# Unused bytes between the SBUF pools of a two-block transformer kernel

## The chip, the cores and the metric

The kernel runs on one core of a Trainium2 chip. The metric is the device time of one execution in microseconds (us), from the start of the program to its end; less is better.

## The reference

The program computes two transformer blocks on 256 tokens of 1024 channels, in float32. Cut to the parts that take the weights:

```python
def first_block(x, ...):
    for layer in range(2):
        h = rmsnorm(x, norm_mix[layer])
        if layer == 0:
            mix = nsa_attention(h, a_w_in, ...)          # compressed, selected and windowed attention
        else:
            kv = rmsnorm(x, kv_norm) @ kv_w              # keys and values of three dilated groups
            mix = dilated_attention(h, b_w_q, k_shared, v_shared, b_w_out, rel_bias)
        x = x + mix
        x = x + swiglu(rmsnorm(x, norm_ffn[layer]), ffn_w_up[layer], ffn_w_down[layer])
    return rmsnorm(x, final_norm)

def second_block(x, mem, ...):
    x = x + 0.5 * swiglu_ffn(rms_norm(x, ffn1_norm), ffn1_w_in, ffn1_w_out)
    h = rms_norm(x, mix_norm)
    ... = jnp.split(h @ w_in, offsets, axis=-1)          # indexed attention, S5 state space, memory attention, gates
    merged = g0 * (o_a @ w_o_a) + g1 * glu(y_s @ w_glu) + g2 * (o_mem @ w_o_m)
    x = x + merged @ w_out
    x = x + 0.5 * swiglu_ffn(rms_norm(x, ffn2_norm), ffn2_w_in, ffn2_w_out)
    return rms_norm(x, final_norm)

def swiglu(h, w_up, w_down):                             # 1024 -> 2 x 2816 -> 1024
    a, b = jnp.split(h @ w_up, 2, axis=-1)
    return (jax.nn.silu(a) * b) @ w_down
```

## The kernel before

The residual stream stays in SBUF, transposed: eight tiles `x0` to `x7` of 128 channels by 256 tokens. A weight product runs on TensorE with float32r operands. To keep float32 accuracy both factors are split into a high and a low part, and each block of 128 input channels costs three matmuls, in `mm3`, lines 222 to 224: high weights by high activations, high weights by low activations, low weights by high activations. Nearly everywhere the weights are the stationary operand (128 by 128) and the activations move (128 by 256). In six products (the values of the attentions and of the memory) it is the other way round: the activations are stationary, and 256 columns of weights move (304 in one product).

Weights come from DRAM in blocks of 8 x 128 rows by 256 columns into the pool `raw` (four buffers, SP's DMA queue, line 172). `split` makes the two parts out of such a block, half a block at a time: ScalarE writes the high part `wh` (line 181), VectorE the low part `wl` (line 182), each into one of four buffers of the pool `wsplit`. The two parts of the activations are in the pool `xsplit` (tags `xh`, `xl`, which the attention outputs `oh`, `ol`, `oah`, `omh` and the merged tiles `mgh`, `mgl` share with the normed stream), with two exceptions. The hidden tiles of a feed-forward, `hh` and `hl`, are in a pool that is opened for that feed-forward (`hid`), and the output tiles of the S5 layer, `ysh` and `ysl`, are in a pool of the mixer.

The stages run in this order: `nsa` (layer 0's attention), `ffn0`, `dil` (layer 1's attention), `ffn1`, `ffn1_2` (the second block's first feed-forward), `mix` (the mixer), `ffn2_2`, and the last norm. Within a stage the order of instructions on an engine is written by a planner from the order in the source and from a priority that the norms are given. The squares' sums of a norm are added on POOL (line 287).

A pool's tiles lie one after the other, and the pools one after the other, in the order in which they are opened. Tiles of a few bytes are rounded up to 32. Per partition, the allocation of the kernel before is, in bytes:

```
const    16512    constants, gains, ones and so on
xres     21728    x0 .. x7                              8 x 1024
xsplit   29920    xh0, xl0, xh1 ..   two buffers each  32 x 1024
raw      62688    weights as loaded                     4 x 8192
wsplit   95456    wh 4 x 4096, wl 4 x 4096
tmp     128224    sqacc, sq, R, and six tiles of 32 (6 x 32 = 192)
then    135584    the pools of nsa, then hid of ffn0, then the pools of dil
late    135584    opened after dil: memory, state space constants (13472 in all)
hid     149056    of ffn1, of ffn1_2 and of ffn2_2, one after the other in time
```

In every `hid` the tiles are 1024 bytes each and start with those of the gate; in `ffn1_2` two tiles of 32 bytes stand ahead of the hidden tiles as well (`gg`, `ss2`). Since a weight tile's blocks are 512 bytes apart, and the tiles of xsplit and hid 1024, the address of a moving tile less that of a weight tile is, modulo 512, the same for all matmuls of a product. Only in the product of 304 columns the blocks of weights are 1216 bytes apart.

Of the kernel before, what the change touches and what calls it, by code (L numbers as in the profile page):

```python
# [18 lines left out]
P = 128  # L19
# [7 lines left out]
AHEAD = 400  # the norms' place before the products that are traced earlier  # L27
BEHIND = 100
WARM = 12
NU = 384  # a row of position biases  # L30
# [86 lines left out]
def flipped(t):  # L117
    """[p, 256] with the tokens of each block of 128 backwards."""
    return blocks(t)[:, :, ::-1]


class Builder:
    def __init__(self, ctx, tc, A):
        self.ctx, self.tc, self.nc, self.A = ctx, tc, tc.nc, A
        nc = self.nc
        e = ctx.enter_context
        self.cpool = e(tc.tile_pool(name="const", bufs=1))
        self.xpool = e(tc.tile_pool(name="xres", bufs=1))
        self.xs_pool = e(tc.tile_pool(name="xsplit", bufs=2))
        self.raw = e(tc.tile_pool(name="raw", bufs=4))  # L130
        self.wsp = e(tc.tile_pool(name="wsplit", bufs=4))
        self.tmp = e(tc.tile_pool(name="tmp", bufs=2))
        self.mm = e(tc.tile_pool(name="mm", bufs=2, space=PSUM))
        self.sc = e(tc.tile_pool(name="sc", bufs=2, space=PSUM))
        self.tr = e(tc.tile_pool(name="tr", bufs=2, space=PSUM))
        self.ov = e(tc.tile_pool(name="ov", bufs=2, space=PSUM))
        self.uid = 0
        self.turn = 0
        self.wide = True

        self.vec = self.cpool.tile([P, NVEC], F32, name="vec")
        self.gains = self.cpool.tile([P, KD * len(GAINS)], F32, name="gains")
        nc.scalar.dma_start(self.gains, A["vec"][:, :KD * len(GAINS)])
        self.con = self.cpool.tile([P, NCON], F32, name="con")
        self.ident = self.con[:, COFF["ident"]:COFF["ident"] + P]
        self.ones = self.cpool.tile([P, P], F32, name="ones")
        nc.vector.memset(self.ones, 1.0)
        self.mhalf = self.cpool.tile([P, 16], F32, name="mhalf")
        nc.gpsimd.memset(self.mhalf, -0.5)
        # the array's clock is released by activity  # L150
        for _ in range(WARM):
            nc.tensor.matmul(self.bank("mm")[:, :P], self.ones, self.ones, start=True, stop=True)

    def rest(self):
        """The small inputs that the first products do not wait for."""
        self.nc.sync.dma_start(self.con, self.A["con"])
        self.nc.sync.dma_start(self.vec, self.A["vec"])

# [26 lines left out]
    def units(self, w, K, c0, cols=256, step=8):  # L185
        """H and L blocks of W[:, c0:c0+cols] as stationary tiles, one list per 128 columns."""
# [13 lines left out]
    def ahead(self, units):  # L200
        """The same units, the first of them loaded and split here."""
        first = next(units)
        return itertools.chain([first], units)

    def wide_units(self, w, K, c0, cols):
        """H and L blocks of W[:, c0:c0+cols] as moving tiles."""
        res = []
        n = 1024 // cols
        for k0 in range(0, K // P, 2 * n):
            kb = min(2 * n, K // P - k0)  # L210
            v = self.load(w, k0 * P, kb, c0, cols)
            for k in range(0, kb, n):
                m = min(n, kb - k)
                res += self.split(v[:, k:k + m, :], m, cols)
        return res

    def mm3(self, ps, pairs):
        """Sum of stationary^T moving over the pairs ((sH, sL), (mH, mL))."""
# [10 lines left out]
    def take(self):  # L229
        """The next bank for a product; while self.wide, the attention's banks are free and take turns."""  # L230
# [6 lines left out]
    def proj(self, unit, X):  # L237
        """[128, 256] in PSUM."""
# [10 lines left out]
    def split_act(self, src, name, k, pool=None, flip=False):  # L249
        """src [128, 256] (SBUF or PSUM) into its two parts; flip: src has each block's tokens backwards."""  # L250
# [14 lines left out]
    def gsplit(self, x, g, k):  # L265
        """The two parts of x g, g [128, 1]."""
# [10 lines left out]
    def sq_add(self, acc, x, k, scale=1.0):  # L277
        """acc: the running sum of squares and the last tile's squares, apart."""
# [10 lines left out]
    def sq_sum(self, ps, acc):  # L289
        """The tokens' sums of squares -> ps [128, 2]."""  # L290
# [4 lines left out]
    def rms(self, ss):  # L295
        """(ss / D + eps) ** -0.5, [128, 2]."""
# [7 lines left out]
    def rows(self, r):  # L304
        """[128, 256] in PSUM: each token's r on every partition."""
# [10 lines left out]
    def rstd(self, acc):  # L316
        """(R [128, 256]: each token's rstd on every partition; r [128, 2]: token-major)."""
# [5 lines left out]
    def norm_all(self, xs, gains):  # L323
        """Splits of every x tile for each gain, and the rstd."""
# [11 lines left out]
    def norm_twice(self, pool, xs, first, second):  # L336
        """The splits for a norm of x normed (x itself becomes that), and both rstds' product.

        x r1 g1 r2 g2: the gains go into the splits, r1 r2 into the product, and
        r2 comes from sum((x g1 r1)^2) = r1^2 sum((x g1)^2)."""  # L340
# [26 lines left out]
    def ffn(self, xs, gain, w_up, w_down, factor, between=None, after=None):  # L367
        nc, tc = self.nc, self.tc
        with tc.tile_pool(name=self.n("hid"), bufs=1) as hp:
            if after:  # L370
# [35 lines left out]
    def bias_rows(self):  # L406
        """Rows u[h, i] = -(bias of distance 255 - i), masks added, into DRAM."""
# [23 lines left out]
    def bias_tile(self, pool, u, row0, heads, tag, bufs):  # L431
        """T[p, h, j] = u[row0 + h, p + j]: the biases of query 127 - p of a block."""
# [6 lines left out]
    def pv_transposed(self, pt_pool, Pm, i, width=384):  # L439
        """Transposes of a head's probabilities [128, 128 | 256] -> [keys, 256 | 128]."""  # L440
# [12 lines left out]
    def pv_mm(self, O, i, V, pt, start, stop):  # L453
        """O[64 i + d, q] += sum over keys; V: (block 0, block 1) [128 keys, 64]."""
# [8 lines left out]
    def key_parts(self, pool, ps, R, dst):  # L463
        """Keys of two groups, each group's two parts on both halves of the array; dst(gp) -> views [128, 2, 128]."""
# [12 lines left out]
    def query_parts(self, pool, ps, Rn, tags):  # L477
        """Queries of two heads, scaled, flipped: a head's two parts on the two halves of the array."""
# [13 lines left out]
    def nsa(self, xs, first):  # L492
# [6 lines left out]
        with ExitStack() as es:  # L499
# [3 lines left out]
            # columns: block, branch (selected, windowed), key  # L503
# [63 lines left out]
            # the compression: keys in columns 0..59, values in columns 64..123 of the array  # L567
# [105 lines left out]
            def values(g, st, j):  # L673
                # normalise and gate
# [146 lines left out]
    def exp_exact(self, pool, dst, x, n, tag):  # L821
        """exp(x) to float32's accuracy, [128, n]."""
# [16 lines left out]
    def s5_consts(self, pool):  # L839
        """Discretised system, per state [128, 8]: rotation (cos, sin), magnitude, input factors."""  # L840
# [45 lines left out]
    def s5_prepare(self, keep):  # L886
        """From the weights alone: rotation tables and input matrices into DRAM, output matrices kept."""
# [5 lines left out]
        self.s5_zc = keep.tile([P, 8, 3, 32], F32, name="s5zc")  # Re C, -Re C, -Im C  # L893
# [6 lines left out]
        with tc.tile_pool(name="s5pre", bufs=1) as pool:  # L900
# [10 lines left out]
            for a in range(2):  # L911
                sl = slice(4 * a, 4 * a + 4)
                # input matrices, zero-padded to all 128 channels of the half
# [18 lines left out]
                # rotation tables cos(theta t), sin(theta t)  # L932
# [28 lines left out]
    def s5(self, pool, ypool, us):  # L961
        """us: two [128 channels, 256] -> gelu(y), split."""
# [3 lines left out]
        for a in range(2):  # L966
# [3 lines left out]
            for b in range(4):  # L970
# [21 lines left out]
                # back: xr = c zr - s zi, xi = s zr + c zi; their sums in the products with C  # L992
# [40 lines left out]
    def mem_keys(self, keep):  # L1033
        """Normed keys of the memory, block-diagonal by head pairs."""
# [14 lines left out]
    def head_ss(self, ps, col, x):  # L1049
        """Sums of squares of both halves of x [128, 256] -> ps[:, block, col:col + 2]."""  # L1050
# [15 lines left out]
    def head_rows(self, pool, r, col):  # L1066
        """[128 (2 x 64), 256] in PSUM: rstd of both heads along the tokens."""
# [9 lines left out]
    def mixer(self, xs):  # L1077
# [4 lines left out]
        with ExitStack() as es:  # L1082
# [64 lines left out]
            # state space  # L1147
            with s5:
                Y = self.s5(sp, mp, us)
            # gates of the second and third branch  # L1150
# [40 lines left out]
            # the 64 best keys of each query  # L1191
# [46 lines left out]
            # first gate, merge branch by branch  # L1238
# [32 lines left out]
def body(tc, A, out, stages=None):  # L1271
    stages = stages or STAGES
    with ExitStack() as ctx:
# [13 lines left out]
        for s in stages:  # L1287
# [8 lines left out]
            elif s == "ffn1":  # L1296
                b.ffn(xs, "norm_ffn1", A["ffn_w_up1"], A["ffn_w_down1"], 1.0, lambda: b.mem_norm(late))
# [3 lines left out]
            elif s == "ffn1_2":  # L1301
# [6 lines left out]
                b.ffn(xs, "ffn1_norm_2", A["ffn1_w_in_2"], A["ffn1_w_out_2"], 0.5, between, "final_norm" if "fin1" in stages else None)  # L1308
# [7 lines left out]
            elif s == "ffn2_2":  # L1316
                b.ffn(xs, "ffn2_norm_2", A["ffn2_w_in_2"], A["ffn2_w_out_2"], 0.5)
            elif s == "fin2":
                b.final(xs, "final_norm_2")
# [4 lines left out]
def _pack(I):  # L1324
    """The inputs as the program reads them: layout only."""
# [73 lines left out]
```

## Time and profile before

| | |
|---|---|
| time, median of 3 runs | 1396.92 us (1394.57 to 1396.95) |
| span of the profiled execution | 1394.9 us |
| TensorE busy (records) | 1372.2 us, 98% |
| weight loads busy (records) | 1301.5 us, 93% |
| VectorE busy | 1022.9 us, 73% |
| ScalarE busy | 745.5 us, 53% |
| POOL busy | 186.4 us, 13% |
| mean granted TensorE clock | 0.992 |

The profile comes from one execution on the chip, whose own time is its span, 1394.9 us from the first to the last instruction; the median of the runs is 2.0 us longer. Records of matmuls overlap, so that TensorE's busy share is no measure of its use: the time from one matmul's start to the next one's start is what a reader should look at. PE is TensorE's matmuls, PEld its weight loads, DVE VectorE, ACT ScalarE, POOL GpSimd.

### The profile page before, as it was taken

The numbers are of one execution on the slowest core, as the hardware profiler recorded it, in microseconds if no ns is written. First come the engines' busy times: TensorE is split into PE (matmuls) and PEld (weight loads), VectorE is DVE, ScalarE is ACT, GpSimd is POOL, SyncE is SP. The second block draws the span as 40 slices with busy tenths as digits, with TensorE's granted clock in tenths as the row PEclk, the third lists the DMA queues.
The fourth block names the chain that finished last, engine by engine and source line by source line (L and its number), as shares of the span: only waits on it lengthen the run. The fifth ranks groups of instructions, "written<-read, shape, count | busy, mean of one in ns | idle before, by whom it ended". The sixth has DMA issues, their size and how long they took to land.

```text
span 1394.9 us, 27445 instructions
## 1 busy us (share of the span) xinstructions
PE 1372.2 (98%) x10880; PEld 1301.5 (93%) x10880; DVE 1022.9 (73%) x2207; ACT 745.5 (53%) x1406; POOL 186.4 (13%) x220
## 2 busy tenths in 40 slices
PE   8999999999999999999999999999999999999997
PEld 8887999999999887999999999999987879999997
DVE  7888677766789775998854877765598797776643
ACT  4677554455668675655443554444334565544442
POOL 4200100001210000423000310001031044000011
PEclk8999999999999999999999999999999999999999
DMA  9751355546755440456655565555744254555451
GB/s 280 246 175 34 112 188 185 182 139 217 234 187 154 123 127 8 160 171 228 215 188 183 170 200 185 178 180 173 233 141 141 66 180 146 171 185 185 154 194 55
DMA packets 227120, 232.76 MB, mean 167 GB/s; under 512 B 5944, under 2 KB 221184, under 8 KB 226992
## 3 DMA queue, kind: packets, MB, share of 16 engines
q1 hardware_dynamic: 223392, 226.14, 51.2%
q10 hardware_dynamic: 3600, 4.88, 1.0%
q8 instruction: 85, 1.39, 0.4%
q14 instruction: 43, 0.35, 0.1%
HBM read 226.69 MB, written 4.30 MB: 166 GB/s over the span
## 4 chain that ended last, share of the span: by engine, by line
PE 56%; DVE 3%; issue 1%; DMA 1%; ACT 1%; POOL 0%; POOLq 0%; DVEq 0%; ACTq 0%
PE mm L222 7%; PE mm L224 7%; PE mm L223 7%; PE sc L223 4%; PE sc L224 4%; PE sc L222 4%; PE tr L222 4%; PE tr L224 4%; PE tr L223 4%; PE ov L223 2%; PE ov L224 2%; PE ov L222 2%; PE ov L999 1%; DVE wl L182 1%; DMA mem<-in_memT_dram 1%
## 5 line engine op out<-in xcount | busy, mean ns | idle before, releaser
L181 ACT ACTIVATE wh<-raw 128x1024 fp32r<-128x1024 f32 (+2 forms) x405 | 418.2, 1036 | 487.7 <-PE mm L223 163.4
L182 DVE TENSOR_TENSOR wl<-raw,wh 128x1024 fp32r<-128x1024 f32 (+2 forms) x405 | 490.0, 1212 | 163.8 <-ACT wh L181 158.7
L222 PE MATMUL mm<-xh,wh 128*128 128x256 f32 x952 | 275.2, 289 | 3.0 <-ACT wh L181 2.9
L224 PE MATMUL mm<-xh,wl 128*128 128x256 f32 x952 | 274.5, 288 | 0.8 <-DVE wl L182 0.8
L223 PE MATMUL mm<-xl,wh 128*128 128x256 f32 x952 | 273.4, 287 | 0.0
L222 PEld LDWEIGHTS mm<-xh,wh 128*128 128x128 f32 x952 | 183.9, 193 | 8.6 <-issue 5.0
L224 PEld LDWEIGHTS mm<-xh,wl 128*128 128x128 f32 x952 | 183.8, 193 | 4.6 <-issue 3.1
L223 PEld LDWEIGHTS mm<-xl,wh 128*128 128x128 f32 x952 | 183.7, 193 | 2.5 <-issue 2.4
L287 POOL TENSOR_TENSOR sqacc<-sqacc,sq 128x256 f32<-128x256 f32 x60 | 60.8, 1014 | 660.3 <-ACT sq L286 350.0
L222 PE MATMUL sc<-xh,wh 128*128 128x256 f32 x464 | 132.0, 285 | 0.9 <-ACT wh L181 0.9
L223 PE MATMUL sc<-xl,wh 128*128 128x256 f32 x464 | 131.8, 284 | 0.0
L224 PE MATMUL sc<-xh,wl 128*128 128x256 f32 x464 | 131.5, 283 | 0.0
L224 PE MATMUL tr<-xh,wl 128*128 128x256 f32 x440 | 125.1, 284 | 0.0
L222 PE MATMUL tr<-xh,wh 128*128 128x256 f32 x440 | 124.8, 284 | 0.0
L223 PE MATMUL tr<-xl,wh 128*128 128x256 f32 x440 | 124.8, 284 | 0.0
L222 PEld LDWEIGHTS sc<-xh,wh 128*128 128x128 f32 x464 | 89.2, 192 | 1.1 <-ACT wh L181 1.1
L223 PEld LDWEIGHTS sc<-xl,wh 128*128 128x128 f32 x464 | 89.3, 192 | 0.0
L224 PEld LDWEIGHTS sc<-xh,wl 128*128 128x128 f32 x464 | 89.1, 192 | 0.0
L224 PEld LDWEIGHTS tr<-xh,wl 128*128 128x128 f32 x440 | 84.5, 192 | 0.2 <-DVE wl L182 0.2
L222 PEld LDWEIGHTS tr<-xh,wh 128*128 128x128 f32 x440 | 84.5, 192 | 0.0
L223 PEld LDWEIGHTS tr<-xl,wh 128*128 128x128 f32 x440 | 84.5, 192 | 0.0
L222 PE MATMUL ov<-xh,wh 128*128 128x256 f32 x224 | 63.7, 284 | 0.0
(482 smaller groups left out, 3472.9 us busy)
## 6 DMA issues: line engine op xcount, KB each, us to landing
raw<-in_ffn_w_up_dram SPq DMA_DIRECT2D x44, 1024.0 KB, 5.3
raw<-in_ffn_w_in_dram SPq DMA_DIRECT2D x44, 1024.0 KB, 5.2
raw<-in_w_in_dram SPq DMA_DIRECT2D x17, 1024.0 KB, 5.3
raw<-in_ffn_w_down_dram SPq DMA_DIRECT2D x16, 1024.0 KB, 5.2
raw<-in_ffn_w_out_dram SPq DMA_DIRECT2D x16, 1024.0 KB, 5.6
raw<-in_b_w_q_dram SPq DMA_DIRECT2D x12, 1024.0 KB, 5.3
raw<-in_a_w_in_dram SPq DMA_DIRECT2D x8, 1024.0 KB, 8.5
bt<-u_scratch SPq DMA_DIRECT2D x28, 256.0 KB, 3.8
```

The costliest lines, as they stand in the source:

```text
L181: nc.scalar.activation(hv, v, AF.Copy)
L182: nc.vector.tensor_tensor(lv, v, hv.bitcast(F32), ALU.subtract)
L222: nc.tensor.matmul(ps, sh, mh, start=(i == 0), stop=False)
L223: nc.tensor.matmul(ps, sh, ml, start=False, stop=False)
L224: nc.tensor.matmul(ps, sl, mh, start=False, stop=(i == n - 1))
L287: nc.gpsimd.tensor_tensor(acc[:, 0], acc[:, 0], s, ALU.add)
L999: nc.tensor.matmul(o, self.s5_zc[:, s, c, :], x, start=(i == 0), stop=(i == 3), tile_position=(0, 32 * b))
```

## The change

Pools of unused bytes are opened ahead of `xsplit` (192 bytes a partition) and ahead of `raw` (320 bytes), and `ffn` gets an argument `skew`: so many unused bytes stand first in that feed-forward's own pool, 320 in `ffn1`, 320 in `ffn1_2`, 416 in `ffn2_2`, none in `ffn0`. Each pad is a tile that POOL sets to zero. All other lines of the diff take away comments.

```diff
+        self.pad(e(tc.tile_pool(name="pad0", bufs=1)), 192)
         self.xs_pool = e(tc.tile_pool(name="xsplit", bufs=2))
+        self.pad(e(tc.tile_pool(name="pad1", bufs=1)), 320)
         self.raw = e(tc.tile_pool(name="raw", bufs=4))
...
+    def pad(self, pool, nbytes):
+
+        self.nc.gpsimd.memset(pool.tile([P, nbytes // 4], F32, name="pad"), 0.0)
...
-    def ffn(self, xs, gain, w_up, w_down, factor, between=None, after=None):
+    def ffn(self, xs, gain, w_up, w_down, factor, between=None, after=None, skew=0):
         nc, tc = self.nc, self.tc
         with tc.tile_pool(name=self.n("hid"), bufs=1) as hp:
+            if skew:
+                self.pad(hp, skew)
             if after:
...
-                b.ffn(xs, "norm_ffn1", A["ffn_w_up1"], A["ffn_w_down1"], 1.0, lambda: b.mem_norm(late))
+                b.ffn(xs, "norm_ffn1", A["ffn_w_up1"], A["ffn_w_down1"], 1.0, lambda: b.mem_norm(late), skew=320)
...
-                b.ffn(xs, "ffn1_norm_2", A["ffn1_w_in_2"], A["ffn1_w_out_2"], 0.5, between, "final_norm" if "fin1" in stages else None)
+                b.ffn(xs, "ffn1_norm_2", A["ffn1_w_in_2"], A["ffn1_w_out_2"], 0.5, between, "final_norm" if "fin1" in stages else None, skew=320)
...
-                b.ffn(xs, "ffn2_norm_2", A["ffn2_w_in_2"], A["ffn2_w_out_2"], 0.5)
+                b.ffn(xs, "ffn2_norm_2", A["ffn2_w_in_2"], A["ffn2_w_out_2"], 0.5, skew=416)
```

## Rows read from the trace of the kernel before

**Rows 1.** The page's first part: busy us, share of the span and instructions by engine.

```profile
PE 1372.2 (98%) x10880; PEld 1301.5 (93%) x10880; DVE 1022.9 (73%) x2207; ACT 745.5 (53%) x1406; POOL 186.4 (13%) x220
```

**Rows 2.** Windows by stretch: start:end, length, busy us (instructions) by engine, clock, DMA share, GB/s.

```profile
0.00:160.00 160.00, 153.72 (x1097) 132.40 (x1098) 124.05 (x381) 100.90 (x263) 33.67 (x52) 0.97 0.54 165
160.00:400.00 240.00, 240.00 (x2034) 240.00 (x2032) 174.42 (x244) 129.94 (x193) 23.12 (x24) 1.00 0.61 193
400.00:560.00 160.00, 156.41 (x1132) 133.75 (x1131) 120.52 (x440) 112.72 (x325) 3.41 (x6) 0.99 0.37 111
560.00:620.00 60.00, 57.72 (x460) 56.99 (x460) 58.06 (x179) 36.16 (x63) 22.10 (x29) 0.96 0.55 178
620.00:980.00 360.00, 360.00 (x3020) 360.00 (x3019) 251.15 (x414) 174.47 (x247) 42.13 (x44) 1.00 0.59 190
980.00:1160.00 180.00, 177.31 (x1261) 151.99 (x1261) 144.81 (x338) 84.27 (x165) 40.73 (x46) 1.00 0.47 146
1160.00:1395.00 235.00, 227.01 (x1889) 226.39 (x1887) 149.88 (x216) 107.08 (x154) 21.23 (x23) 0.99 0.49 157
```

**Rows 3.** Windows of steady weight products, TensorE alone.

```profile
180.00:280.00 100.00, 100.00 (x835) 1.00 0.59 190
300.00:340.00 40.00, 40.00 (x355) 1.00 0.64 205
...
715.00:755.00 40.00, 40.00 (x335) 1.00 0.52 167
...
925.00:955.00 30.00, 30.00 (x258) 1.00 0.58 184
...
1330.00:1380.00 50.00, 50.00 (x419) 1.00 0.37 123
```

**Rows 4.** Timeline of TensorE in the s5 products: start, length in us.

```profile
1143.61 0.28 PE L223 MATMUL mm<-ysl,wh 128*128 128x256 f32 x1
...
1144.78 0.28 PE L224 MATMUL mm<-ysh,wl 128*128 128x256 f32 x1
```

**Rows 5.** Timeline of TensorE in the product of 304 columns.

```profile
43.47 0.30 PE L222 MATMUL mm<-wh,xh 128*128 128x304 f32 x1
...
43.88 0.31 PE L222 MATMUL mm<-wh,xh 128*128 128x304 f32 x1
...
44.31 0.31 PE L222 MATMUL mm<-wh,xh 128*128 128x304 f32 x1
...
44.73 0.30 PE L222 MATMUL mm<-wh,xh 128*128 128x304 f32 x1
```

**Rows 6.** Windows over the span: TensorE's instructions that read xh, then xl.

```profile
0.00:1395.00 1395.00, 808.55 (x4352) 0.99 0.53 167
...
0.00:1395.00 1395.00, 620.06 (x2176) 0.99 0.53 167
```

**Rows 7.** The same for the full-pace stretches, xh and then xl.

```profile
160.00:400.00 240.00, 171.63 (x949) 1.00 0.61 193
620.00:980.00 360.00, 229.19 (x1267) 1.00 0.59 190
1160.00:1395.00 235.00, 127.29 (x704) 0.99 0.49 157
...
160.00:400.00 240.00, 134.20 (x474) 1.00 0.61 193
620.00:980.00 360.00, 179.29 (x633) 1.00 0.59 190
1160.00:1395.00 235.00, 99.79 (x352) 0.99 0.49 157
```

**Rows 8.** Timeline of TensorE in ffn1's down product.

```profile
740.28 0.28 PE L222 MATMUL sc<-hh,wh 128*128 128x256 f32 x1
740.39 0.29 PE L223 MATMUL sc<-hl,wh 128*128 128x256 f32 x1
740.52 0.28 PE L224 MATMUL sc<-hh,wl 128*128 128x256 f32 x1
```

## The prediction

> **What bounds the kernel now.** I read first the page's engine totals and granted clock, to see which engine carries the time: TensorE is recorded busy 98% of the span [rows 1], and its granted clock is 0.96 to 1.00 in every stretch [rows 2], which is the upper level, 2.4 GHz. That share alone proves little, because a matmul record lasts about 284 ns while the next one starts long before it ends. So the second view is the table by stage [rows 2]. The reader is to see two kinds of stretches. In three of them (160 to 400, 620 to 980, 1160 to 1395 us; feed-forward, projections) TensorE and its weight loads fill the stretch, while VectorE needs 174.4 of 240, 251.2 of 360 and 149.9 of 235 us (73, 70 and 64%) and ScalarE less: nothing but TensorE's own pace sets the time there, apart from the last few us, which are the output's. In the other four (attention, the start, 560 to 620) the weight loads have holes, and VectorE is at 78, 75, 97 and 80%.
>
> The third view is the pace itself: windows that hold nothing but weight products of 256 columns [rows 3]. A window's count includes about two matmuls that began before it. So 180 to 280 gives 100 / (835 - 2) = 120.0 ns from start to start, 300 to 340 gives 40 / (355 - 2) = 113.3, 715 to 755 gives 120.1, 925 to 955 gives 117.2 and 1330 to 1380 gives 119.9. The first is an up product (moving tiles in xsplit), the other four are the down products of ffn0, ffn1, ffn1_2 and ffn2_2. These four run the same lines on the same shapes, with the same granted clock of 1.00. The fastest has the highest VectorE share of them (26.3 of 40 us against 19.5 of 40 in ffn1), so it isn't the lighter load that makes it fast. What differs is where the hidden tiles lie.
>
> **Distances.** I call distance the address of the moving tile minus that of the weight tile, modulo 512 bytes; within each pool all these tiles are a multiple of 512 bytes apart. From the allocation of the kernel before (pool starts are in the section on the kernel): x tiles 29,920 - 95,456, distance 0; ffn0 135,584 - 95,456 = 40,128, distance 192; ffn1 and ffn2_2 149,056 - 95,456 = 53,600, distance 352; ffn1_2 has 64 bytes of small tiles ahead, distance 416. The s5 output tiles have distance 288 and run ten intervals in 1144.78 - 1143.61 us, 117 ns [rows 4]. So the trace gives pace against distance: 0: 120.0; 192: 113.3; 288: 117; 352: 120.0; 416: 117.2. Five points are no law, but equal code with unequal pace is strong evidence that distance counts. A weaker witness: in the product of 304 columns the weight rows are the moving side, and block k lies 1,216 k bytes on, distances 192, 384, 0 in turn. Three matmuls each take 0.41, 0.43 and 0.42 us [rows 5]: the same order, 137 against 140 ns, half the effect.
>
> **The change, part by part.** The two constant pads move xsplit by 192 bytes and everything from raw on by 512. Nothing else of the compute moves.
>
> Part 1, x tiles: distance 0 becomes 192 - 512, which is 192 modulo 512, the one that ran at 113.3 in ffn0. I take that pace: 6.6 ns saved each (with 120.0 and 113.4, the second rounded towards less gain). The matmuls that read xh and xl are 4352 and 2176 [rows 6]; 288 of them (six products of 48, the values) have the weights moving. In the full-pace stretches there are 949 + 474 + 1267 + 633 + 704 + 352 = 4379 [rows 7], less four of those value products (three of layer 1, one of the memory; 192): 4187. They save 4187 x 6.6 = 27.6 us, undiluted, since at 113.4 VectorE's share there would rise only by a factor of 1.06, to 77%.
> The rest is 6528 - 288 - 4187 = 2053, and 720 more by the code (attention outputs and merged tiles, also in xsplit: 384 + 192 + 96 + 48), together 2773. Some of the 720 sit in full-pace stretches, which this leaves out in favour of caution. All of them would save 18.3 us; none would if VectorE and ScalarE set those stretches. Weight products fill TensorE's waits there, and in 560 to 620 VectorE has 58.1 of 60 us, which excludes a gain in that stretch. I take half, 9.2 us, between 0 and 18.3.
>
> Part 2, the hidden tiles with a skew: 528 matmuls (22 x 8 x 3) in each of three products. ffn1 goes from 352 to 352 + 320 - 512 = 160, ffn1_2 from 416 to 224, ffn2_2 from 352 to 256; ffn0 stays at 192. No row shows 160, 224 or 256. The best known pace, 113.4, would save (6.6 + 3.8 + 6.6) x 0.528 = 9.0 us; the worst, 120.0, would lose 2.8 x 0.528 = 1.5 us in ffn1_2 and nothing in the others. Reading straight lines between neighbours gives 114.5, 114.7 and 116.0, a gain of 6.3 us. Against that stands that 288 and 416, 128 apart, are equal: if the pattern repeats each 128 bytes, 160 is 416's, 224 is 352's and 256 is 0's, and the three together give nothing. I take the middle, 3.2 us.
>
> Part 3, the value products: 240 of 256 columns go from 0 to 320, which lies between 288 and 352; 113.4 saves 1.6 us and 125 costs 1.2. I take 0. The s5 products keep 288.
>
> Part 4, the zeroing: two memsets on POOL at the start, of 48 and 80 columns, and three of 80 to 104. The one memset of before there, 16 columns, is not on anybody's path, and POOL is idle at 87% [rows 1]. A skew memset waits until the tiles under it are read, and the squares' sums are queued behind it on POOL; those need the residual stream, which is later than these reads. If it did delay a norm, the norm's 0.1 to 0.2 us memset would show once per feed-forward, under 1 us in all. Taken as 0.
>
> Sum: 27.6 + 9.2 + 3.2 = 40.0 us off the profiled span of 1394.9, so 1354.9. The runs shown have a median of 1396.92, 2.0 above that span, so about 1357.
>
> **A rule that speaks against it.** The traced row is the pace, 120.0 against 113.3 at the same clock [rows 3]. The Trainium skill, page "SBUF — State Buffer", section "Who interferes with whom", gives TensorE two independent read ports, one for the moving operand and one for weight loads, and says that PE never waits on anyone; by it distance could not matter and the time would stay at 1397. The trace of before doesn't agree, unless something else slows three of four equal products.
>
> **Rivals.**
> No effect (0.06): the pace of ffn0 comes from something that went with its place in the program, not from its distance. For it: the 304-column rows show only half the effect, and ffn0 is one sample. Against it: 353 intervals in a row, and s5 with 117 as well. Time 1397.
> Half pace (0.10): x tiles land at 117.2 as in ffn1_2, since xh and xl are 2,048 bytes apart and ffn0's hh and hl 1,024; or VectorE, at 97% in 560 to 620, binds in more places. 2.8 ns x (4187 + half of 2773 = 5574) = 15.6 us, so 1381.
> Slower (0.06): distance alone doesn't fix the pace. In ffn1 the intervals alternate, 0.11 and 0.13 us in one output [rows 8]: a locked pattern that has a slow phase. If the 2,048 bytes between xh and xl lock the x products into that phase for half their intervals more than now, 0.005 us x 5574 = 28 us are added, so 1425. It decides as soon as the up products' pace is above 120.0.
> Faster still (0.02): the pace falls below 113, since 192 needn't be the best distance; at 4 ns less, 4 x 5574 = 22 us come off as well, 1335. No row shows such a pace. The Trainium skill, page "TensorE: Matmul & The Clock Gate", section "Back-to-back issue gap", gives 262 cycles for 256 columns, an estimated 109 ns at 2.4 GHz.
>
> **How the numbers follow.** Forecast 0.76: x tiles near 113.4. Its bounds are the parts' bounds: all of it, 27.6 + 18.3 + 9.0 + 1.6 = 56.5 us, gives 1340; the least, 27.6 - 1.5 - 1.2 = 24.9, gives 1372. The range goes a little into the half-pace case, to 1380. About 0.2% (2.8 us) is what a measurement of this kernel can tell from no change. Faster 0.76 + 0.10 + 0.02 = 0.88, same 0.06, slower 0.06.
>
> **What would show it.** Right: windows of up products hold 6% more matmuls (about 884 in 100 us), ffn0's down product keeps its 113.3, TensorE's granted clock stays. Part 2 is read from the paces of the three skewed down products, each by itself. The attention stretches show whether half was a fair share: their length after against 160, 160, 60 and 180 us. Wrong: an up pace of 120 (no effect), of 117 (half), or a pace of 113 with new waits of TensorE on the splits of lines 181 and 182 (VectorE binds).

## The result, and the profile after

The changed kernel takes 1376.04 us (median of 4 runs, 1374.24 to 1378.42) against 1396.36 of the kernel before: a ratio of 0.986, interval 0.9848 to 0.9872. It is 20.3 us faster, about half of the 40.0 us that were forecast. The profiled execution has a span of 1372.4 us, 22.5 less than the 1394.9 of before.

The page's first part, which answers to [rows 1]; TensorE's matmul records and its weight loads became 23 and 24 us shorter in sum, and the busy times of the other engines changed by at most 0.3%:

```profile
PE 1349.5 (98%) x10880; PEld 1277.6 (93%) x10880; DVE 1020.7 (74%) x2207; ACT 743.8 (54%) x1406; POOL 186.8 (14%) x225
```

The order of the instructions on TensorE, ScalarE and SP is the same as before, so every matmul can be matched with itself. From the start of the same matmul to the start of the same matmul, between those that stood at the edges of [rows 2]:

```
stretch before   before    after    shorter by
   0 -  160      159.0     156.9     2.0
 160 -  400      240.1     238.5     1.6
 400 -  560      160.1     158.5     1.6
 560 -  620       59.9      58.5     1.3
 620 -  980      360.1     349.6    10.5
 980 - 1160      179.9     176.9     3.0
1160 - 1395      228.7     226.1     2.6
```

Nearly half of the gain is in one stretch, and the two other full-pace stretches, with the same kind of work, give 1.6 and 2.6 us. The windows that answer to [rows 3] tell why (TensorE alone: count, clock, DMA share, GB/s; the four pairs of lines are an up product and its down product, of ffn0, ffn1, ffn1_2, ffn2_2):

```profile
180.00:280.00 100.00, 100.00 (x851) 1.00 0.57 184
300.00:340.00 40.00, 40.00 (x342) 1.00 0.51 165
640.00:690.00 50.00, 50.00 (x443) 1.00 0.69 227
710.00:750.00 40.00, 40.00 (x344) 1.00 0.61 196
830.00:890.00 60.00, 60.00 (x532) 1.00 0.62 199
910.00:945.00 35.00, 35.00 (x298) 1.00 0.52 167
1190.00:1290.00 100.00, 100.00 (x852) 1.00 0.56 184
1310.00:1355.00 45.00, 45.00 (x377) 1.00 0.36 115
```

Less the two that began before each window, the up products run at 117.8, 113.4, 113.2 and 117.6 ns, all four with x tiles at distance 192. So there are two paces at one distance. Start to start, a triple of matmuls takes 340 ns (3 x 113.3) or 353.3 (3 x 117.8): of 6,286 triples of x matmuls that nothing holds up, 6,240 lie within 5 ns of one of the two. The down product of ffn0, whose distance the change leaves at 192, went from 113.3 to 117.6. Of the skewed ones, 160 runs at 117.0 (before, at 352: 120.1), 224 at 118.2 (before, at 416: 117.2), 256 at 120.0 (before, at 352: 119.9).

Where a stretch changes its pace can be seen in the timeline. Here ffn0's up product goes over from 113 to 118 (start, length in us; L228 to L230 are the lines 222 to 224 of before, L314 is the norm's row of rstds):

```profile
172.42 0.28 PE L229 MATMUL tr<-xl,wh 128*128 128x256 f32 x1
172.53 0.28 PE L230 MATMUL tr<-xh,wl 128*128 128x256 f32 x1
172.65 0.60 PE L314 MATMUL ov<-con,rr 128*128 128x128 f32 x4
173.01 0.36 PE L228 MATMUL tr<-xh,wh 128*128 128x256 f32 x1
173.21 0.28 PE L229 MATMUL tr<-xl,wh 128*128 128x256 f32 x1
173.33 0.28 PE L230 MATMUL tr<-xh,wl 128*128 128x256 f32 x1
173.44 0.28 PE L228 MATMUL tr<-xh,wh 128*128 128x256 f32 x1
173.56 0.28 PE L229 MATMUL tr<-xl,wh 128*128 128x256 f32 x1
```

Before the four foreign matmuls the starts are 0.11 us apart, behind them 0.12, at the same distance; and so it stays for 177 us, through the rest of the up product and nearly all of the down product behind it, until two other matmuls come in. That gave the theory (H, lock): at such a distance the stream of loads and matmuls has two steady patterns, a restart after other work decides which, and it is kept until the next interruption. Rivals were a longer period of the addresses (D: everything behind raw moved by 512 bytes as well) and an outside disturbance (N).

Matmul by matmul, the time from start to start summed over the span: products with moving tiles in xsplit 26.1 us shorter where nothing waits, and 3.6 longer at waits and interruptions; ffn1's down product 1.4 shorter; ffn0's 2.3 and ffn1_2's 0.5 longer; ffn2_2's equal; products with moving weights 1.6 shorter; all other matmuls 0.1 longer. Together 22.6, the sum of the table.

### The profile page after: what moved, and what is told of

Its sections match the earlier page's. It is cut to its first block, busy times and chain, and to the rows that moved or that the text cites. A ratio compares the mean times of both kernels' runs of the same rounds, so it can differ in the third digit from the quotient of the medians.

```text
span 1372.4 us, 27451 instructions
## 1 busy us (share of the span) xinstructions
PE 1349.5 (98%) x10880; PEld 1277.6 (93%) x10880; DVE 1020.7 (74%) x2207; ACT 743.8 (54%) x1406; POOL 186.8 (14%) x225
## 4 chain that ended last, share of the span: by engine, by line
PE 55%; DVE 4%; issue 1%; ACT 1%; DMA 1%; POOL 0%; POOLq 0%; DVEq 0%; ACTq 0%
PE mm L228 7%; PE mm L230 7%; PE mm L229 7%; PE tr L230 4%; PE sc L230 4%; PE sc L229 4%; PE tr L228 4%; PE sc L228 4%; PE tr L229 4%; PE ov L229 2%; PE ov L230 2%; PE ov L228 2%; PE ov L1007 1%; DVE wl L188 1%; DMA mem<-in_memT_dram 1%
## 5 line engine op out<-in xcount | busy, mean ns | idle before, releaser
L228 PE MATMUL mm<-xh,wh 128*128 128x256 f32 x952 | 271.9, 286 | 1.6 <-ACT wh L187 1.4
L230 PE MATMUL mm<-xh,wl 128*128 128x256 f32 x952 | 271.2, 285 | 1.0 <-DVE wl L188 1.0
L229 PE MATMUL mm<-xl,wh 128*128 128x256 f32 x952 | 270.1, 284 | 0.0
L228 PEld LDWEIGHTS mm<-xh,wh 128*128 128x128 f32 x952 | 182.1, 191 | 7.1 <-issue 5.0
L230 PEld LDWEIGHTS mm<-xh,wl 128*128 128x128 f32 x952 | 181.2, 190 | 4.8 <-issue 3.1
L228 PE MATMUL sc<-xh,wh 128*128 128x256 f32 x464 | 129.8, 280 | 1.9 <-ACT wh L187 1.9
L230 PE MATMUL sc<-xh,wl 128*128 128x256 f32 x464 | 129.3, 279 | 0.0
L228 PE MATMUL tr<-xh,wh 128*128 128x256 f32 x440 | 123.2, 280 | 0.4 <-ACT wh L187 0.4
L230 PE MATMUL tr<-xh,wl 128*128 128x256 f32 x440 | 123.3, 280 | 0.2 <-DVE wl L188 0.2
L228 PEld LDWEIGHTS sc<-xh,wh 128*128 128x128 f32 x464 | 87.7, 189 | 2.1 <-ACT wh L187 2.1
L230 PEld LDWEIGHTS sc<-xh,wl 128*128 128x128 f32 x464 | 87.2, 188 | 0.0
L228 PEld LDWEIGHTS tr<-xh,wh 128*128 128x128 f32 x440 | 83.4, 189 | 0.6 <-ACT wh L187 0.6
L230 PEld LDWEIGHTS tr<-xh,wl 128*128 128x128 f32 x440 | 83.1, 189 | 0.4 <-DVE wl L188 0.4
L228 PE MATMUL ov<-xh,wh 128*128 128x256 f32 x224 | 62.6, 280 | 0.0
```

The lines of the kernel that those rows point to most:

```text
L228: nc.tensor.matmul(ps, sh, mh, start=(i == 0), stop=False)
L229: nc.tensor.matmul(ps, sh, ml, start=False, stop=False)
L230: nc.tensor.matmul(ps, sl, mh, start=False, stop=(i == n - 1))
```

## The experiments

### The same kernel again

No edit.

> The changed kernel, unaltered. Theory H (lock): at distance 192 the stream has two steady paces, 113.3 and 117.8 ns; which one it takes is settled by exact timing when it restarts after other work, so in a second execution some of the long products change sides (of the up products of ffn0, ffn1, ffn1_2 and ffn2_2, which ran at 117.8, 113.3, 113.3 and 117.8, at least one differs), and products without an interruption between them stay on one side. Rival D (address): the pace follows from the addresses alone, so every product repeats its pace within 0.2 ns, time 1376 within 2.

1377.2 us. ffn1's up product and its down product:

```profile
640.00:690.00 50.00, 50.00 (x427) 1.00 0.62 200
710.00:750.00 40.00, 40.00 (x340) 1.00 0.50 158
```

ffn1's up product, 443 in 50 us in the first execution, has 427 in this one (117.6 ns), with the same program and the same addresses. Its down product at 160 went from 117.0 to 118.3. The other three up products kept their side (851, 532 and 851). D falls: addresses alone don't set the pace. What differed between the two executions when ffn1 began is not shown.

### Everything 1024 bytes on, and no skews

```diff
-        self.pad(e(tc.tile_pool(name="pad0", bufs=1)), 192)
+        self.pad(e(tc.tile_pool(name="pad0", bufs=1)), 704)
...
-    ... skew=320), skew=320), skew=416)
+    ... skew=0), skew=0), skew=0)
```

> First pad 704 instead of 192 bytes, no skews: distances of the x tiles and of ffn0 stay 192, and weights and everything behind them lie 1024 bytes on from the kernel before, not 512. Rival D with a period of 1024: what changed ffn0's down product from 113.3 to 117.8 is that everything moved by 512, so it is back at 113.3 here, and the up products are all at 113.3: 6960 x 6.6 = 46 us less than before, about 1351. Theory H: a mixture of 113.3 and 117.8 again, about 1370 to 1382; ffn1 and ffn2_2 down (352) at 120.0, ffn1_2 down (416) at 117.3.

1376.96 us.

```profile
180.00:280.00 100.00, 100.00 (x851) 1.00 0.58 189
300.00:340.00 40.00, 40.00 (x342) 1.00 0.55 177
...
710.00:750.00 40.00, 40.00 (x335) 1.00 0.48 157
...
910.00:945.00 35.00, 35.00 (x300) 1.00 0.59 193
...
1310.00:1355.00 45.00, 45.00 (x377) 1.00 0.44 140
```

ffn0 stays at 117.8 and 117.6, so the 512 bytes were not what took its 113.3 away. The unskewed down products are back at 120.1, 117.4 and 120.0. Without any skew the time is that of the full change (1376.04 and 1377.2), so the skews are worth nothing that one run can show.

### Two sweeps of the distance

```diff
-        self.pad(... "pad0" ..., 192)      # sweep a: none;  sweep b: 64
-        self.pad(... "pad1" ..., 320)      # sweep a: none;  sweep b: 448
-    skews 0, 320, 320, 416                 # sweep a: 384, 480, 32, 288;  sweep b: 352, 256, 480, 128
```

The lines are shortened, and the last one sums up four calls.

> No pads ahead of xsplit and raw; skews 384, 480, 32, 288 give the down products of ffn0, ffn1, ffn1_2, ffn2_2 the distances 64, 320, 448, 128. Theory H with a repeat each 128 bytes: the first three are 113.3 or 117.8 each, the last 120.0; up products 120.0; time 1386 to 1397. Rival D with a period of 512: paces between those of the neighbours measured at 0, 192, 288, 352, 416: about 118, 119, 118 and 116.

1393.53 us. The down products at 64, 320, 448 and 128:

```profile
300.00:350.00 50.00, 50.00 (x427) 1.00 0.61 198
715.00:760.00 45.00, 45.00 (x385) 1.00 0.55 180
...
920.00:960.00 40.00, 40.00 (x356) 1.00 0.57 186
1325.00:1370.00 45.00, 45.00 (x382) 1.00 0.49 157
```

Paces 117.6, 117.5, 113.0 and 118.4.

> Pads 64 and 448: x tiles at distance 64; skews 352, 256, 480, 128 give the down products the distances 32, 96, 384, 480. Theory H with a repeat each 128 bytes: up products at 113.3 or 117.8 by product; down products 117.3 (as 160 and 416), 118 to 120 (as 224 and 352), 120.0 (as 0 and 256), 118 to 120; time 1365 to 1385. Rival D with a period of 512: 64 is a distance of its own, nearer to 0 than to 192, so the up products run at one pace of about 118 and the time is about 1384 or more.

1381.51 us. An up product at 64, and the down products at 32, 96, 384 and 480:

```profile
180.00:280.00 100.00, 100.00 (x851) 1.00 0.57 184
300.00:340.00 40.00, 40.00 (x336) 1.00 0.48 156
...
705.00:755.00 50.00, 50.00 (x419) 1.00 0.59 191
...
910.00:955.00 45.00, 45.00 (x381) 1.00 0.56 178
...
1315.00:1360.00 45.00, 45.00 (x382) 1.00 0.44 143
```

117.8; then 119.8, 119.9, 118.7 and 118.4. The long up products were all at 117.8 here, 113.3 came up in short ones only. Together: 64, 192, 320 and 448, which are equal modulo 128, show no paces but one pair (64 and 192 both of them, 320 and 448 one each so far), and D's interpolation (118, 119, 118, 116) is wrong. The repeat of 128 bytes holds for this pair and not for the rest: 0 and 256 give 120.0, 128 and 384 give 118.4 and 118.7; 32 gives 119.8, while 160, 288 and 416 give 117 to 118. So three of the expected paces missed: 120.0 at 128 and at 384, and 117.3 at 32. Whether those too are several patterns of one distance is open; 160 has shown two.

It could be the address of the moving tile alone that counts. The products with moving weights speak against it: there the weights move, at the same address modulo 512 before and after, and only the x tiles, now the stationary operand, have been shifted. A product of layer 1's values, nine intervals before and nine in the changed kernel:

```profile
385.72 0.28 PE L222 MATMUL tr<-wh,xh 128*128 128x256 f32 x1
386.80 0.28 PE L222 MATMUL tr<-wh,xh 128*128 128x256 f32 x1
...
382.77 0.28 PE L230 MATMUL tr<-wh,xl 128*128 128x256 f32 x1
383.79 0.28 PE L230 MATMUL tr<-wh,xl 128*128 128x256 f32 x1
```

That is 120.0 and 113.3 ns; the others went from 120.0 to 117.7 or 113.3. In the product of 304 columns it is the weights' place that varies, with the x tiles at one address modulo 512, and there the triples take 415, 425 and 420 ns in turn before. So the addresses of both operands count. That only their difference counts is not shown: in every run the weights' buffers were moved by multiples of 512 bytes.

### Distances in steps of 8 and 16 bytes

```diff
-                    h = hp.tile([P, S], F32R, ...)
+                    h = hp.tile([P, S + 128], F32R, ...)[:, fine:fine + S]      # and l the same way
```

The skew of ffn2_2 is 352 here, so that 8 bytes more make 200.

> The changed kernel with the hidden tiles of ffn0, ffn1 and ffn2_2 used from an offset of 16, 16 and 8 bytes (spaced 1536 bytes), so that their down products stand at 208, 176 and 200; the up products stay at 192. Theory H: the set of paces follows the distance in steps finer than 32 bytes; 200 and 208 still have 113.3 as one of theirs, 176 lies between 160 (117.3 or 118.7) and 192. Rival D (steps of 32 or 64 bytes): 200 and 208 behave as 192, 176 as 160.

1378.86 us. The down products at 208, 176 and 200:

```profile
300.00:340.00 40.00, 40.00 (x338) 1.00 0.51 170
700.00:750.00 50.00, 50.00 (x422) 1.00 0.59 192
...
1310.00:1355.00 45.00, 45.00 (x378) 1.00 0.46 152
```

119.0, 119.0 and 119.7: none at 113.3, although the up products ahead of the first and last were at 117.8. So 8 and 16 bytes off 192 the pair is lost. The hidden tiles also stand 1536 bytes apart here and not 1024, a multiple of 512 as well, and no run has this spacing at 192: that it is the 8 bytes and not the spacing is not shown. The expectation that 200 and 208 keep 113.3 missed, and so did the rival's, that they behave as 192.

### Kicks: one foreign matmul in the stream

```diff
+                    if c == 0 and mp:
+                        w = (1, 8, 16, 32, 48, 64, 80, 96, 112, 128)[mp - 1]
+                        nc.tensor.matmul(self.bank("ov")[:, :w], self.ones, self.ones[:, :w], start=True, stop=True)
                     pa = self.proj(next(ua), X)
```

> The same with float32 kicks on a constant tile of ones, 1 to 128 columns wide, whose weights and moving columns come from other addresses. Theory H: flips at kicks, and the side after a kick need not be that of the kick of the same order in the other kernel; 40 x 0.15 to 0.35 us of extra work, 6 to 14 us; time 1368 to 1392. Rival N: as there.

1378.19 us. ffn0's up product, a stretch of 9 us behind each of the kicks with 1, 8, 16, 32 and 48 columns:

```profile
179.00:188.00 9.00, 9.00 (x82) 1.00 0.69 227
190.00:199.00 9.00, 9.00 (x79) 1.00 0.69 227
201.50:210.50 9.00, 9.00 (x82) 1.00 0.69 228
213.00:222.00 9.00, 9.00 (x81) 1.00 0.67 221
224.00:233.00 9.00, 9.00 (x79) 1.00 0.68 226
```

81 and 82 are the fast pattern (2 + 9 / 0.1133), 79 the slow one. Over all 40 kicks: from the slow pattern every one, of whatever width, led to the fast one (20 of 20); from the fast pattern all led to the slow one (17 of 17) but those of 32 columns, which kept the fast (3 of 3). So the side isn't drawn by chance: in these 40 kicks the pattern ahead and the width fix the pattern behind. Nor does the side change by itself: in the ten traces with x tiles at 192, each of the 476 undisturbed stretches of x products (24 matmuls or more, no start over 126 ns after the one ahead) shows one of the two patterns only. N falls.

With float32r kicks on the product's own operands (`u[0][0]`, `X[0][0][:, :w]`, w from 8 to 240):

> The changed kernel with one extra matmul ahead of the second to eleventh block of each feed-forward's up product, on the next product's own operands, 8 to 240 columns wide, result unused: 40 kicks at unchanged addresses. Theory H (lock): the pace between two kicks (48 x 2 matmuls) is either 113.3 or 117.8 and flips at kicks only; some widths set the same side in all four feed-forwards. 40 x 0.06 to 0.12 us of extra work, 3 to 5 us; time 1365 to 1385. Rival N (noise: the side is drawn by something outside the program, such as refresh or the transfers): flips fall within undisturbed stretches as well, or kicks don't move the side at all.

1383.43 us. Here, too, the side changed only behind kicks and other interruptions: 224 columns left the fast pattern behind them in all four feed-forwards, 240 and 160 the slow one. But 192, each time from the slow pattern, led once to the fast and three times to the slow, and 8 and 64 didn't always do the same from the slow pattern either; in all three ffn0 was the odd one. With these kicks the width and the pattern ahead don't fix the outcome, and what else does is open. The time was at the upper end of what was expected, since more kicks ended on the slow side.

### A single kick

```diff
-                b.ffn(xs, "norm_ffn0", A["ffn_w_up0"], A["ffn_w_down0"], 1.0)
+                b.ffn(xs, "norm_ffn0", A["ffn_w_up0"], A["ffn_w_down0"], 1.0, kick=(1,))      # 32 columns ahead of block 2
```

> The changed kernel with a single extra matmul in the whole program: float32, 32 columns, result unused, ahead of the second block of ffn0's up product. In the kernel with float32 kicks the widths 1, 8, 16, 64, 96 and 128 turned 117.8 into 113.3 and turned 113.3 into 117.8; width 32 left 113.3 four times in four. Theory H: from the kick on ffn0's up product runs at 113.3 (30 of 33 eighths of about 1000 matmuls), and its down product, which follows without an interruption at the same distance, too: (950 + 528) x 4.45 = 6.6 us less up to the end of ffn0, less 0.2 for the kick. Rival N (noise): ffn0 stays at 117.8 in both, as in all four kernels with x tiles at 192 or 64 and no kick.

1369.04 us, 7.0 less than the changed kernel's median. Matmul by matmul against the profiled execution of the changed kernel, ffn0 is 6.4 us shorter (4.0 in the up product, 2.3 in the down product), the 6.4 that were expected; the other stretches differ both ways. ffn0's up and down product:

```profile
185.00:280.00 95.00, 95.00 (x841) 1.00 0.58 188
300.00:340.00 40.00, 40.00 (x355) 1.00 0.55 177
```

113.2 and 113.3. One matmul of no use, at about 180 us, sets the pace of the next 165 us.

### Kicks at distance 0

The kernel before, with the kick of 32 columns ahead of blocks 2, 5 and 8 of each feed-forward.

> The kernel before (x tiles at distance 0) with the same kick ahead of blocks 2, 5 and 8 of each feed-forward, 12 kicks. Theory H: distance 0 has one steady pace, so every up product stays at 120.0 and the kicks cost 0.2 us each; time 1396 to 1401. If 0 has another pace too, kicks show it.

1399.43 us. Between ffn0's kicks (two of the stretches), and its down product:

```profile
185.00:210.00 25.00, 25.00 (x211) 1.00 0.60 193
216.00:246.00 30.00, 30.00 (x252) 1.00 0.64 207
...
300.00:350.00 50.00, 50.00 (x443) 1.00 0.64 211
```

119.6 and 120.0: at distance 0 the kick leaves the pace as it is and only costs time: in the trace the starts around a kick take 0.46 us in place of 0.24, about 0.22 us for each. The 4.0 us above the median of before (1395.48) are more than these 2.7; single executions differ by as much as the rest. So it isn't the kick that makes the stream fast; it chooses between the patterns that the distance has. The down product at 192, entered from 120.0, is at 113.4 again, as in the kernel before.

### Two widths in turn

```diff
+                        w = 32 if mp % 2 else 48
+                        nc.tensor.matmul(self.bank("ov")[:, :w], self.ones, self.ones[:, :w], start=True, stop=True)
```

> The changed kernel with kicks ahead of blocks 2 to 11 of the up products of ffn0 and ffn2_2, 32 columns ahead of the even ones and 48 ahead of the odd ones; ffn2_2's down product at 192. Theory H, with the two widths' effect as seen so far (32 leads to 113.3 from either pace, 48 turned 113.3 into 117.8 four times in four): the blocks alternate, 2, 4, 6, 8, 10 at 113.3 and 3, 5, 7, 9, 11 at 117.8, in both feed-forwards, and the down products carry on at 117.8. Rival: the kick only breaks a pattern and the next one is drawn by chance: about half of the 20 blocks on the side named.

1380.92 us. ffn0's blocks 2 to 5, and the down products of ffn0 and ffn2_2:

```profile
182.00:191.00 9.00, 9.00 (x82) 1.00 0.68 225
193.00:202.00 9.00, 9.00 (x79) 1.00 0.70 228
204.50:213.50 9.00, 9.00 (x82) 1.00 0.69 230
216.00:225.00 9.00, 9.00 (x79) 1.00 0.69 227
...
300.00:350.00 50.00, 50.00 (x427) 1.00 0.60 197
1310.00:1360.00 50.00, 50.00 (x427) 1.00 0.47 153
```

All 20 blocks were on the side named beforehand, and the last side, 117.8, was carried into both down products (117.6).

### The faster version

```diff
+                    if c == 0 and mp in kick:
+                        nc.tensor.matmul(self.bank("ov")[:, :32], self.ones, self.ones[:, :32], start=True, stop=True)
...
-    ffn0: skew 0      ffn1: skew 320                      ffn1_2: skew 320                      ffn2_2: skew 416
+    ffn0: kick=(1,)   ffn1: skew=352, kick=(1, 2, 3, 4)   ffn1_2: skew=288, kick=(1, 2, 3, 4)   ffn2_2: skew=352, kick=(1,)
```

The last two lines sum up the arguments of the four calls.

> All four down products at distance 192 (skews 0, 352, 288, 352) and ten kicks of 32 columns: ahead of block 2 in ffn0 and ffn2_2, ahead of blocks 2 to 5 in ffn1 and ffn1_2. Theory H: up products at 113.3 after the kicks and down products at 113.3, carried over: against the changed kernel 4.2 us each in the up products of ffn0 and ffn2_2, 0 to 3.5 in ffn1's, and 2.3, 2.4, 2.6 and 3.5 in the four down products, less 10 x 0.23 for the kicks: 17 to 20 us less, 1356 to 1360, a ratio to the kernel before of 0.971 to 0.974. Rival N: no more than the down products' share by chance, 1370 or more.

1356.14 us (median of 5, 1354.31 to 1359.63), a ratio to the kernel before of 0.9718, interval 0.9705 to 0.9732: about 20 us below the changed kernel, 39 below the kernel before. Its profiled execution, the slowest of the five, still has a slow piece, ffn1 from 655 us on. A matmul that waited for VectorE's low part of the weights began it:

```profile
655.12 0.28 PE L228 MATMUL tr<-xh,wh 128*128 128x256 f32 x1
655.24 0.28 PE L229 MATMUL tr<-xl,wh 128*128 128x256 f32 x1
655.75 0.39 PE L230 MATMUL tr<-xh,wl 128*128 128x256 f32 x1 [0.24 <-DVE wl L188]
655.98 0.28 PE L228 MATMUL tr<-xh,wh 128*128 128x256 f32 x1
```

Not every wait does that: 3 us earlier, at 652.26, a shorter one for the same split (0.25 us from start to start, against 0.51 here) left the fast pattern as it was.

A kick more ahead of ffn1's block 9, and one ahead of each of the seven output and down products:

> The kernel with ten kicks, and one more ahead of block 9 of ffn1 (where a wait for VectorE's split put it back to 117.8) and one ahead of each of the seven output and down products. Theory H: ffn1's last blocks and its down product (about 210 + 528 matmuls) and the merge's output product (192) at 113.3: (738 + 192) x 4.45 = 4.1 us less where they had been at 117.8, less 8 x 0.23 = 1.8 for the kicks: 1351 to 1357, most likely 1354.

1358.19 us (1356.8 to 1358.59), 0.9732, interval 0.9718 to 0.9745. In its profile ffn1's last blocks and all four down products are at 113.3, but the merge's output product stayed at 117.8: its kick, at 1124.7 us, came 10 us ahead of its first matmul, with waits between. The time missed the expected 1351 to 1357 and isn't below that of the ten kicks; the two intervals overlap, so which of the two is faster isn't settled.

## Why the prediction was wrong

The direction, the bound and the view were right: the pace of the weight products sets the time, it depends on the distance, and nothing else had to give way. The step that failed is in part 1: "distance 0 becomes 192 - 512, which is 192 modulo 512, the one that ran at 113.3 in ffn0. I take that pace". The one row at 192 was one of two steady patterns of that distance. After the change 44% of the undisturbed triples of x matmuls were at the fast one and 56% at the slow: 26.1 us, less 3.6 at waits, against the 36.8 that the two sums of part 1 had. The measured 1376.04 lies within the stated 1340 to 1380, but beyond the 1372 that the forecast case gave at the least: the few us by which the range reached towards the half-pace case held it, and not the mechanism. Two long products, ffn0's and ffn2_2's, were slow in all executions of the kernels with x tiles at 192 and no kick; ffn1's was fast in one and slow in three others.

The same reading failed a second time in part 2: "ffn0 stays at 192" was taken for "ffn0 stays at 113.3". It lost 2.3 us, since it carries on the pattern of the up product ahead of it. The three skewed products together gave 0.9 us (1.4 - 0.5 + 0.0) in place of 3.2; the doubt written beside it, that 160, 224 and 256 could give nothing together, was the better guess. Part 3 gave 1.6 us in place of 0. Part 4 was right to be 0: the five pads' memsets took 0.8 us in all, and no engine waited for them.

The four stretches with attention became 7.9 us shorter (2.0 + 1.6 + 1.3 + 3.0) against 9.2. That this is near is luck in part: the x matmuls saved some 4.2 ns each over the whole program (44% of 6.7 and 56% of 2.2), and half of 2773 at 4.2 ns would be 5.8 us, so that a saving taken too high met a share taken too low. In 560 to 620, where no gain was thought possible, 1.3 us came off.

With the fast pattern chosen on purpose ten kicks and 192 everywhere give 1356.14, against the 1357 of the prediction. So close a match is luck: that kernel pays for its kicks, has better distances for the down products, and in its trace 70% of the undisturbed triples of x matmuls are fast, not all. But it does show that most of the missing half was the choice between two patterns, and not VectorE, the transfers or the clock. Of the rivals, "half pace" came nearest, with 117.8 in place of 117.2, for a reason that it hadn't: the 2,048 bytes between xh and xl have nothing to do with it, as the same tiles run at either pace, and ffn0's hidden tiles, 1,024 apart, run at 117.6 too. The rival that was nearest in mechanism is "slower": it says that distance alone doesn't fix the pace and speaks of a locked pattern with a slow phase, but it had that phase above 120.0 and its time at 1425.

Open remain the cause behind the distances (whether TensorE's two reads meet somewhere), whether 8 bytes matter by themselves, why a kick of 32 columns leads to the fast pattern from either side, and what in a restart differs from one execution to the next.

## What to carry to other kernels

A row that shows a pace once shows that the pace is possible, not that the layout gives it: look for the same layout twice, and at what came just before. Where matmuls follow each other for hundreds of microseconds, compare the time from start to start (not the busy share) between stretches of equal shapes; a few ns on each are worth tens of us. Where such a stream had several steady paces, as here, addresses chose the set and the restart chose the member, and a matmul of no use was a cheap way to choose.

## What the runs showed of the hardware

In these traces the stream of weight loads and 256-column matmuls locks into steady patterns: 113.3 or 117.8 ns each at distance 64 modulo 128, 120.0 at 0, at the same granted clock of 1.00; at other distances it ran between these. The two at 64 modulo 128 differ by 4.4 ns, 3.9%, and one stayed for up to 177 us until another matmul broke in. A wait of 0.24 us on one matmul therefore cost far more than itself in the version with ten kicks: about 95 triples and the whole down product behind it, some 800 matmuls x 4.45 = 3.6 us.

The Trainium skill, page "SBUF — State Buffer", section "Who interferes with whom", gives TensorE two read ports, one for the moving operand and one for weight loads, calls them independent and says that PE never waits on anyone. As a statement on pace the traces don't agree: with the x tiles moved from distance 0 to 192 and the same instructions, their matmuls went from 120.0 to 117.8 or 113.3 ns each. Whether the two reads get in each other's way there, no run shows.
